# Attention pipeline: evictions of keys and queries at the head of a step, conversions of values behind the result, products dealt nine and six

## The chip, the core and the metric

The kernel runs on one core of a Trainium2 chip. TensorE (PE in the profile; PEld is its weight load) multiplies matrices into PSUM, VectorE (DVE) and ScalarE (ACT) read PSUM and work element by element, GpSimd (POOL) works on SBUF and issues some of the DMAs, SyncE (SP) issues the other DMAs. Each engine runs its own queue strictly in order; a semaphore makes one wait for another. The metric is the device time of one execution in microseconds. Before the change it was 2920.61 us, the median of three runs (2917.56 to 2922.97).

## The reference

Two layers of a backbone over 1024 latent tokens and 256 context tokens, 1024 channels each. The first layer mixes with Fourier groups and long convolutions, the second with neighbourhood attention; each ends in a SwiGLU feed-forward part. Only the attention of the second layer matters here. 16 heads of 64 channels; a query sees an 8 x 16 window of keys on a grid of 16 rows by 64 columns, with a bias by relative position, and all context keys:

```python
s_loc = einsum("bcqhd,bicjhd->bhcqij", q_r, k_b) * scale + bias
s_loc = where(col_ok, s_loc, -inf)
s_ctx = einsum("bcqhd,bjhd->bhcqj", q_r, kc) * scale
p = softmax(concatenate([s_loc, s_ctx], axis=-1))
o = einsum("bhcqij,bicjhd->bcqhd", p_loc, v_b) + einsum("bhcqj,bjhd->bcqhd", p_ctx, vc)
```

## The kernel before, in words

Operands are kept as a high and a low half in a narrower type, so that one product of the reference becomes three matmuls (high by high, high by low, low by high).

The attention has 64 items: 8 pairs of heads (`pr`), two halves of the rows (`hf`), four groups of 16 columns (`c`). An item has 128 queries, 384 local keys and 256 context keys for each of its two heads. One step of the loop over `k` in `attention` works on three items at once:

- `attn_scores` and `attn_softmax` for item k + 1: twelve score matmuls into four PSUM banks named `sc`; then on DVE the smallest context score (L2072), the sum with the bias and its extremum (L2074), on ACT the exponentials (L2078, L2080). The context half is split by ACT (L2086) and POOL (L2087) and transposed by a DMA on SyncE's queue (L2088).
- `attn_turn` for item k: PE transposes the local half (L2098) into two banks named `tr`; `turned` copies it out, high half on ACT (L2107), low half on DVE (L2110).
- `attn_values` for item k - 1: thirty matmuls with the values, into the unused half of a score bank of item k + 1 (`free`); then DVE takes the reciprocal of the softmax sum (L2138) and multiplies (L2139) into `osb`. Only then is that score bank free for the scores of the next step. Every fourth step `attn_send` transposes a finished `osb` (L2150), splits it (L2152 on ACT, L2153 on DVE) and stores it. From item 52 on, the context half is transposed on PE too, in `attn_late`.

Between these pieces PE does the projections of the next pair: `attn_prep` is a generator that yields after every three matmuls into one of two accumulators `pq`. Five accumulations of 24 matmuls make a pair: two of the keys (512 columns), the context keys (256), two of the queries (512). `fetch(target)` draws from this generator until the work drawn reaches the target. For the last eight steps and beyond, the generator is the output projection (`first_part`).

What ACT and DVE have to do for the projections is not done on the spot but put in a list, `self.later`, by `later(work)`: the **evictions** of a finished accumulator (`key`: copy on ACT L300 and rest on DVE L302; `context_key`: L1946 and L1947; `query`: L1951 and L1952), and the **conversions** of a loaded group of values (`value`: POOL memset L1973, ACT L1974, DVE L1975; no DMA). An eviction is listed when the generator is drawn from again after its last product; a conversion at a fixed count of products. `flush()` empties the list.

The loop lies in a `manual_schedule`: the queues of PE, ACT, DVE and POOL hold the instructions in the order in which the code issues them.

Of the kernel before, what the change touches and what calls it, by code (L numbers as in the profile page):

```python
# [201 lines left out]
class Builder:  # L202
# [1705 lines left out]
    def attn_prep(self, pr, u):  # L1908

        nc = self.nc  # L1910
        kh, kl = self.S4(F32R), self.S4(F32R)
        kc = self.S2(F32R)
        qs, vt, staged = {}, [], {}
        loads, turns = (1, 5, 10, 16, 22), (12, 16, 22, 28, 33)
        step = 0

        def lin(wh, wl, pc, view=lambda x: x):
            nonlocal step, acc
            yield None
            acc = self.PQ()  # L1920
            for kb in range(KB):
                for w, part in ((wh, 0), (wh, 1), (wl, 0)):
                    self.mm(acc[:, :WID[pc]], w[:, kb * P:(kb + 1) * P], view(u.ap(part, kb, pc)),
                            kb == 0 and w is wh and part == 0, kb == KB - 1 and w is wl)
                step += 1
                for c in range(5):
                    if step == loads[c]:
                        load(c)
                    if step == turns[c]:
                        later(lambda c=c: value(c))  # L1930
                yield WID[pc] / 1024

        def by_chunk(x):
            return x.rearrange("p (r h c) -> p h r c", r=8, h=4)

        def later(work):
            if pr == 0:
                work()
            else:
                self.later.append(work)  # L1940

        def key(acc, cols):
            self.split(acc, kh[:, cols], kl[:, cols])

        def context_key(acc):
            nc.scalar.mul(kc[:, :256], acc[:, :256], -1.0)  # L1946
            nc.vector.scalar_tensor_tensor(kc[:, 256:], acc[:, :256], -1.0, kc[:, :256].bitcast(F32), op0=MUL, op1=SUB)  # L1947

        def query(acc, pc):
            qh, ql = qs[pc] = self.S2(F32R), self.S2(F32R)  # L1950
            nc.scalar.mul(qh, acc, self.qinv)  # L1951
            nc.vector.scalar_tensor_tensor(ql, acc, self.qinv, qh.bitcast(F32), op0=MUL, op1=SUB)  # L1952

        def load(c):
            st = staged[c] = self.T()
            if c < 4:
                src = self.vd[0:LAT].rearrange("(g r w) c -> r w g c", g=4, r=4)
                for r in range(4):
                    self.ld(st[r * 32:r * 32 + 32].rearrange("p (g c) -> p g c", g=4),
                            src[r, KSTART[c]:KSTART[c] + 32, :, pr * P:(pr + 1) * P])  # L1960
            else:
                self.ld(st[:, :256].rearrange("p (j c) -> p j c", j=2),
                        self.vd[LAT:LAT + CTX, pr * P:(pr + 1) * P].rearrange("(j p) c -> p j c", j=2))

        def value(c):
            st = staged.pop(c)
            w = 512 if c < 4 else 256
            n = w // 64
            t = self.S4(F16, 2048) if c < 4 else self.S2(F16, 1024)
            v = t[:, :66 * n].rearrange("p (k c) -> p k c", c=66)  # L1970
            lo = t[:, 66 * n:130 * n]
            src = st[:, :w].rearrange("p (k c) -> p k c", c=64)
            nc.gpsimd.memset(v[:, :, 64:65], 1.0)  # L1973
            nc.scalar.activation(v[:, :, :64], src, AF.Copy, scale=self.vs)  # L1974
            nc.vector.scalar_tensor_tensor(lo.rearrange("p (k c) -> p k c", c=64), src, self.vs, v[:, :, :64],  # L1975
                                           op0=MUL, op1=SUB)
            vt.append((v, lo))

        acc = None
        wk = self.halves_of("wk", 0) if pr == 0 else self.aw  # L1980
        for pc in (0, 1, 2):
            if pc == 1:
                wq = self.halves_of("wq", pr)
            yield from lin(*wk, pc)
            later((lambda acc=acc: context_key(acc)) if pc == 2 else
                  (lambda acc=acc, pc=pc: key(acc, slice(pc * 512, pc * 512 + 512))))
        for pc in (0, 1):
            if pc == 1 and pr < 7:
                self.aw = self.halves_of("wk", pr + 1)
            yield from lin(*wq, pc, by_chunk)  # L1990
            later(lambda acc=acc, pc=pc: query(acc, pc))
        self.prep[pr] = (qs, (kh, kl), (kc[:, :256], kc[:, 256:]), vt)
        yield 0.1

    def attention(self, u, fill):
        self.prep, self.osb, self.aw, self.later, self.turns = {}, {}, None, [], []
        self.od = [[self.DR([P, LAT], F16) for _ in range(2)] for _ in range(8)]
        self.accumulators(sc=4, tr=2, pq=2)
        n = sum(x or 0 for x in self.attn_prep(0, u))
        prep = (x for pr in range(1, 9) for x in (self.attn_prep(pr, u) if pr < 8 else fill))  # L2000
        items = [(pr, hf, c) for pr in range(8) for hf in (0, 1) for c in range(4)]
        state = [{} for _ in items]
        done = 0

        def piece(step, k):
            if 0 <= k < 64:
                step(state[k], *items[k])

        def fetch(target):
            nonlocal done  # L2010
            while done < target:
                done += next(prep) or 0

        def flush():
            while self.later:
                self.later.pop(0)()

        for k in range(2):
            piece(self.attn_bias, k)
        e = mybir.EngineType  # L2020
        with self.tc.manual_schedule(engines={e.PE, e.Activation, e.DVE, e.Pool}):
            for k in range(-1, 65):
                piece(self.attn_bias, k + 3)
                piece(self.attn_send, k - 2)
                piece(self.attn_scores, k + 1)
                piece(self.attn_turn, k)
                piece(self.attn_softmax, k + 1)
                flush()
                fetch((k * 3 + 8.5) * n / 24)
                free = state[k + 1]["free"] if k + 1 < 64 else self.SC()[:, 256:]  # L2030
                if 0 <= k - 1 < 64:
                    self.attn_values(state[k - 1], *items[k - 1], free)
                piece(self.attn_late, k)
                flush()
                fetch((k * 3 + 10) * n / 24)
            flush()
            piece(self.attn_send, 63)
        for _ in prep:
            pass
        self.accumulators(pp=6, pq=2)  # L2040
# [524 lines left out]
```

## Time and profile before

| | us |
|---|---|
| median of three runs | 2920.61 |
| the profiled execution, its own time | 2916.52 |
| its span in the trace | 2914.8 |
| six whole rounds of eight steps (1815.4 to 2124.1) | 51.4 each |
| PE, DVE, ACT busy in the round 1918.3 to 1969.7 | 48.67, 34.50, 31.53 |
| DMA share and PE clock granted in that round | 0.65, 1.00 |

The profiled execution is one run; its span is the time between its first and last instruction, and 1.7 us lie around it. A busy engine is one that has an instruction in work; PE's matmuls overlap, so the profile models their ends. The attention loop is some 410 us of the span.

### The profile page before, as it was taken

The page shows a single profiled execution, that of the slowest core. Times are in us where ns is not written, and L with a number is a line of the kernel's source. Part 1 is how long each engine was busy: PE and PEld are TensorE (multiplying, and loading weights), DVE is VectorE, ACT ScalarE, POOL GpSimd, SP SyncE. Part 2 cuts the span into 40 slices and gives each one's busy share as a digit, 9 for nine tenths or more (in the row PEclk, how much of TensorE's full clock was granted, in tenths as well). Part 3 has the DMA queues.
Part 4 walks back from the last instruction along what each step waited for, and adds up shares of the span by engine and source line. Part 5 has one row for each costly group of instructions (what it writes and reads, how often), then busy time and mean ns, then how long its engine had stood idle before and what let it go on. Part 6 is the DMA issues. An engine that isn't in the chain of part 4 may idle for free. (4 is left out here: it accounts for less than half of the span.)

```text
span 2914.8 us, 46336 instructions
## 1 busy us (share of the span) xinstructions
PE 2761.7 (95%) x16419; PEld 1686.2 (58%) x16419; DVE 2078.8 (71%) x3857; ACT 1619.3 (56%) x2857; POOL 593.3 (20%) x977
## 2 busy tenths in 40 slices
PE   6989999999989999999999999999999999999998
PEld 3755557888879544444555844666665444444554
DVE  4778767575467898877886766666675778765755
ACT  4674325454675676654465655666663467554543
POOL 1012013354121121112120012333331012112000
PEclk8999999999999999999999999999999999999999
DMA  7574435359695655556994897666664656424753
GB/s 258 189 272 169 157 114 169 108 175 307 248 356 176 208 217 195 210 195 255 321 321 161 300 336 276 147 164 154 164 189 163 231 215 239 154 99 179 235 189 124
DMA packets 323362, 607.58 MB, mean 208 GB/s; under 512 B 89910, under 2 KB 131576, under 8 KB 323130
## 3 DMA queue, kind: packets, MB, share of 16 engines
q1 hardware_dynamic: 254682, 387.53, 40.6%
q0 software_dynamic: 66144, 212.91, 20.6%
q10 hardware_dynamic: 2304, 4.20, 0.4%
q8 instruction: 128, 2.10, 0.3%
q14 instruction: 104, 0.85, 0.1%
HBM read 455.33 MB, written 135.53 MB: 203 GB/s over the span
## 5 line engine op out<-in xcount | busy, mean ns | idle before, releaser
L1462 PE MATMUL ps<-s,s 128*128 128x512 f16 x2244 | 507.4, 381 | 8.6 <-ACT tk L1467 4.2
L1462 PEld LDWEIGHTS <-s 128*128 128x128 f16 x2640 | 258.6, 98 | 330.7 <-issue 25.2
L296 PE MATMUL ps<-s,wh 128*128 128x256 f32 (+3 forms) x1764 | 400.8, 330 | 12.4 <-ACT wh L300 5.4
L1231 ACT ACTIVATE s<-s,c 128x512 f16<-128x512 f32 (+1 forms) x324 | 233.6, 752 | 149.2 <-DMA s<-d 73.5
L1232 DVE SCALAR_TENSOR_TENSOR s<-s,c,s 128x512 f16<-128x512 f32 (+1 forms) x324 | 247.2, 793 | 90.1 <-ACT s L1231 89.3
L1679 PE MATMUL ps<-s 128*128 128x512 f16 (+2 forms) x1308 | 303.6, 378 | 2.0 <-DVE s L1232 2.0
L296 PE MATMUL pq<-s,wh 128*128 128x512 f16 (+1 forms) x988 | 273.6, 355 | 5.0 <-DMA wh<-d 3.0
L296 PE MATMUL ps<-s,wl 128*128 128x256 f32 (+3 forms) x882 | 263.6, 331 | 2.5 <-DVE wl L302 1.2
L1679 PEld LDWEIGHTS <-s 128*128 128x128 f16 x1536 | 148.5, 98 | 179.0 <-issue 6.8
L296 PEld LDWEIGHTS <-wh 128*128 128x128 f16 x1664 | 159.6, 99 | 152.6 <-issue 13.6
L287 POOL DMA_DIRECT2D d<-s x201 | 108.7, 541 | 640.6 <-DVE s L1523 182.5
L348 ACT CAST mat<-cs 128x1024 fp32r<-128x1024 f16 (+2 forms) x120 | 111.5, 934 | 137.7 <-PE ps L296 56.6
L296 PEld LDWEIGHTS ps<-s,wh 128*128 128x128 f32 x1088 | 177.1, 192 | 18.1 <-ACT wh L300 5.7
L296 PE MATMUL ps<-s,mat 128*128 128x512 f32 x696 | 180.5, 405 | 4.6 <-DVE s L302 4.3
L1462 PE MATMUL ps<-s,wh 128*128 128x512 f16 x608 | 182.2, 379 | 1.7 <-DVE g L1476 1.3
L296 PE MATMUL pq<-s,wl 128*128 128x512 f16 (+1 forms) x494 | 172.3, 354 | 0.0
L296 PE MATMUL sc<-s,s 128*128 128x65 f16 (+3 forms) x2688 | 153.2, 233 | 16.6 <-DVE s L2139 13.3
L296 PEld LDWEIGHTS <-s 128*128 128x128 f16 x2400 | 113.2, 98 | 80.0 <-issue 11.5
L296 PEld LDWEIGHTS ps<-s,mat 128*128 128x128 f32 x696 | 133.3, 194 | 38.5 <-DVE s L302 5.5
L1264 ACT ACTIVATE t<-s 128x1024 bf16<-128x1024 f32 (+1 forms) x164 | 141.5, 863 | 12.3 <-DVE c L483 8.5
L2107 ACT CAST s<-tr 128x384 f16<-128x384 f32 (+1 forms) x140 | 62.9, 490 | 137.2 <-PE tr L2098 136.9
L296 PEld LDWEIGHTS <-wl 128*128 128x128 f16 x832 | 82.2, 99 | 81.5 <-issue 2.8
(435 smaller groups left out, 5555.6 us busy)
## 6 DMA issues: line engine op xcount, KB each, us to landing
s<-d SPq DMA_DIRECT2D x294, 256.0 KB, 4.4
d<-s POOLq DMA_DIRECT2D x157, 256.0 KB, 3.5
s<-in_down SPq DMA_DIRECT2D x154, 256.0 KB, 5.1
s<-in_ada_w POOLq DMA_DIRECT2D x48, 512.0 KB, 4.7
s<-in_gate SPq DMA_DIRECT2D x46, 512.0 KB, 3.9
s<-in_up SPq DMA_DIRECT2D x46, 512.0 KB, 4.3
d<-g POOLq DMA_DIRECT2D x87, 256.0 KB, 3.5
d<-tk POOLq DMA_DIRECT2D x82, 256.0 KB, 4.5
```

The costliest lines, as they stand in the source:

```text
L287: self.last_ldr = self.nc.gpsimd.dma_start(out, in_).ins
L296: return self.nc.tensor.matmul(o, l, r, start=st, stop=sp).ins
L348: self.nc.scalar.copy(m, st)
L1231: nc.scalar.activation(hi, src, AF.Copy, scale=scale)
L1232: nc.vector.scalar_tensor_tensor(lo, src, scale, hi, op0=MUL, op1=SUB)
L1264: self.nc.scalar.activation(junk[:, :t.shape[1]], t, AF.Abs, scale=2.0 ** -15, accum_out=st[:, k:k + 1])
L1462: nc.tensor.matmul(ps, x[:, sl], y, start=first and j == 0 and x is wh and y is xh, stop=j == 3 and x is wl, skip_group_check=True)
L1679: m = nc.tensor.matmul(acc[j][:, c0:c1], x[:, sl], y[:, xs], start=first and k == 0, stop=last and k == 2, skip_group_check=True)
L2107: self.nc.scalar.copy(t[:, :w], ps[:, :w])
```

## The change

Three edits in the order of a step, and a second list.

- The conversions of values go to a list of their own, `self.casts`.
- `flush(self.later)`, now the evictions alone, opens a step, ahead of `attn_send` and the scores. Before, the list was emptied behind the softmax and once more at the end of the step.
- `flush(self.casts)` stands behind `attn_values`, ahead of `attn_late`.
- The first `fetch` of a step goes to `k * 3 + 8.9` instead of `k * 3 + 8.5`; the second is unchanged.

```diff
                     if step == turns[c]:
-                        later(lambda c=c: value(c))
+                        later(lambda c=c: value(c), self.casts)
...
-        def later(work):
+        def later(work, queue=self.later):
             if pr == 0:
                 work()
             else:
-                self.later.append(work)
+                queue.append(work)
...
-        def flush():
-            while self.later:
-                self.later.pop(0)()
+        def flush(queue):
+            while queue:
+                queue.pop(0)()
...
             for k in range(-1, 65):
                 piece(self.attn_bias, k + 3)
+                flush(self.later)
                 piece(self.attn_send, k - 2)
                 piece(self.attn_scores, k + 1)
                 piece(self.attn_turn, k)
                 piece(self.attn_softmax, k + 1)
-                flush()
-                fetch((k * 3 + 8.5) * n / 24)
+                fetch((k * 3 + 8.9) * n / 24)
                 free = state[k + 1]["free"] if k + 1 < 64 else self.SC()[:, 256:]
                 if 0 <= k - 1 < 64:
                     self.attn_values(state[k - 1], *items[k - 1], free)
+                flush(self.casts)
                 piece(self.attn_late, k)
-                flush()
                 fetch((k * 3 + 10) * n / 24)
-            flush()
+            flush(self.later)
+            flush(self.casts)
```

Two lines come in ahead of the loop, so L2072 to L2153 of before are L2074 to L2155 of the changed kernel.

Where the conversions and evictions stand is seen on DVE. Here is its queue from the end of the softmax of one step to the beginning of the next, in the step of a round in which a conversion of values and the second half of the keys meet (`tr` are the transposed weights, `t` the loaded values, `sc` a score bank with a result or with scores, `pq` a projection). Before:

```order
L2110 TENSOR_TENSOR s_4177_19681<-tr_19668,s_4177_19681 128x384
L2110 TENSOR_TENSOR s_4178_19683<-tr_19672,s_4178_19683 128x384
L1975 SCALAR_TENSOR_TENSOR s_4181_19697<-t_19418,c_17518,s_4181_19697 128x512
L2138 RECIPROCAL st_19457<-sc_19654 128x2
L2139 TENSOR_TENSOR s_4183_19711<-sc_19654,st_19457 128x128
L302 TENSOR_TENSOR s_4110_19310<-pq_19485,s_4109_19309 128x512
L2072 TENSOR_REDUCE st_19791<-sc_19769 128x1
```

The same place now:

```order
L2112 TENSOR_TENSOR s_4177_19681<-tr_19668,s_4177_19681 128x384
L2112 TENSOR_TENSOR s_4178_19683<-tr_19672,s_4178_19683 128x384
L2140 RECIPROCAL st_19457<-sc_19654 128x2
L2141 TENSOR_TENSOR s_4182_19710<-sc_19654,st_19457 128x128
L1975 SCALAR_TENSOR_TENSOR s_4183_19743<-t_19386,c_17518,s_4183_19743 128x512
L302 TENSOR_TENSOR s_4110_19310<-pq_19485,s_4109_19309 128x512
L2074 TENSOR_REDUCE st_19791<-sc_19769 128x1
```

The two instructions of the division have passed the conversion; the eviction L302 stands between the conversion and the reduction, as it did.

Three steps later a query and the short last conversion stood together ahead of the division. DVE's queue there, before:

```order
L2110 TENSOR_TENSOR s_4085_19141<-tr_19128,s_4085_19141 128x384
L2110 TENSOR_TENSOR s_4086_19143<-tr_19132,s_4086_19143 128x384
L1952 SCALAR_TENSOR_TENSOR s_4090_19158<-pq_18956,c_13658,s_4089_19157 128x512
L1975 SCALAR_TENSOR_TENSOR s_4091_19161<-t_18895,c_17518,s_4091_19161 128x256
L2138 RECIPROCAL st_18931<-sc_19114 128x2
L2139 TENSOR_TENSOR s_4039_18851<-sc_19114,st_18931 128x128
```

Now:

```order
L2112 TENSOR_TENSOR s_4087_19145<-tr_19132,s_4087_19145 128x384
L2112 TENSOR_TENSOR s_4088_19147<-tr_19136,s_4088_19147 128x384
L2140 RECIPROCAL st_18931<-sc_19118 128x2
L2141 TENSOR_TENSOR s_4038_18850<-sc_19118,st_18931 128x128
L1975 SCALAR_TENSOR_TENSOR s_4091_19202<-t_18893,c_17518,s_4091_19202 128x256
```

The conversion has gone behind the division, and the query's L1952 has left this place for the head of the step, ahead of the reduction L2074.

The dealing of the products is seen on PE, at the end of the first fetch of a step (`pq` products, then the values into `sc`). Before, the sixth product is the last:

```order
L296 LDWEIGHTS wl_19482
L296 MATMUL pq_19816<-s_3363_15495,wl_19482 128x512
L296 LDWEIGHTS s_4177_19681
L296 MATMUL sc_19769<-s_4037_18837,s_4177_19681 128x65
L296 LDWEIGHTS s_4177_19681
```

Now three more follow, up to the ninth:

```order
L296 LDWEIGHTS wl_19482
L296 MATMUL pq_19812<-s_3363_15495,wl_19482 128x512
L296 LDWEIGHTS wh_19481
L296 MATMUL pq_19812<-s_3368_15512,wh_19481 128x512
L296 LDWEIGHTS wh_19481
L296 MATMUL pq_19812<-s_3368_15512,wh_19481 128x512
L296 LDWEIGHTS wl_19482
L296 MATMUL pq_19812<-s_3368_15512,wl_19482 128x512
L296 LDWEIGHTS s_4177_19681
L296 MATMUL sc_19769<-s_4039_18883,s_4177_19681 128x65
```

Counted over a round, four steps had six products ahead of the values and nine behind and now have nine and six. The step of the context keys, whose products have 256 columns and half the length, had nine and fifteen and now has twelve and twelve. The other three keep six and six.

More of the change, by code (lines that the diff above doesn't have):

```diff
@@ L1995, in attention @@
     def attention(self, u, fill):
-        self.prep, self.osb, self.aw, self.later, self.turns = {}, {}, None, [], []
+        self.prep, self.osb, self.aw, self.turns = {}, {}, None, []
+        self.later, self.casts = [], []
         self.od = [[self.DR([P, LAT], F16) for _ in range(2)] for _ in range(8)]
```

## The prediction

> **What bounds the kernel now.** I began with the page: the whole execution, and how busy each engine is.
>
> ```profile
> span 2914.8 us, 46336 instructions
> PE 2761.7 (95%) x16419; PEld 1686.2 (58%) x16419; DVE 2078.8 (71%) x3857; ACT 1619.3 (56%) x2857; POOL 593.3 (20%) x977
> ```
>
> TensorE (PE) is 95% busy, so a change of order can only win what holds PE up. The change lies in attention alone, which by the first and last score products runs from about 1805 to 2215 us. Second view: what PE waited for in that stretch (columns: who waited, for whom, us in total, times, longest).
>
> ```profile
> PE sc L296 <- DVE s L2139: 13.3, 21, 0.9
> PE tr L2150 <- DVE s L2139: 3.5, 6, 0.6
> PE sc L296 <- ACT t L2078: 3.3, 11, 0.4
> ```
>
> Nearly everything is a wait for L2139, the division of a result by its softmax sum on VectorE (DVE). It stands 21 + 6 times; with seven pairs of heads being prepared that is three or four times in each round of eight steps. Third view: the timeline of such a round (start us, length, engine, line; in brackets the idle time ahead and what ended it). A round is the distance between the first and the fifth row here, 1918.30 - 1866.85 = 51.45 us.
>
> ```profile
> 1866.85 1.06 PE L296 MATMUL sc<-s,s 128*128 128x65 f16 x30 [0.23 <-ACT t L2078]
> ...
> 1916.40 0.74 DVE L2072 TENSOR_REDUCE st<-sc 128x1 f32<-128x256 f32 x2
> ...
> 1917.06 0.61 DVE L2074 CUSTOM_DVE_ANT_0 g<-sc,g,st 128x384 f32<-128x384 f32 x1
> ...
> 1917.78 0.47 ACT L2078 ACTIVATE t<-sc,st 128x256 f32<-128x256 f32 x1 [0.17 <-DVE st L2074]
> ...
> 1918.30 1.06 PE L296 MATMUL sc<-s,s 128*128 128x65 f16 x30 [0.23 <-ACT t L2078]
> ...
> 1920.78 1.13 DVE L1975 SCALAR_TENSOR_TENSOR s<-t,c,s 128x512 f16<-128x512 f32 x1 [1.63 <-ACT s L1974]
> ...
> 1920.93 0.79 PE L296 MATMUL sc<-s,s 64*128 64x256 f32 x7
> ...
> 1921.83 0.16 DVE L2138 RECIPROCAL st<-sc 128x2 f32<-128x2 f32 x1
> ...
> 1922.02 0.29 DVE L2139 TENSOR_TENSOR s<-sc,st 128x128 f32<-128x128 f32 x1
> 1922.23 0.68 DVE L302 TENSOR_TENSOR s<-pq,s 128x512 fp32r<-128x512 f32 x1
> ...
> 1922.46 0.77 PE L296 MATMUL sc<-s,s 64*128 64x384 f32 x5 [0.74 <-DVE s L2139]
> 1922.83 0.74 DVE L2072 TENSOR_REDUCE st<-sc 128x1 f32<-128x256 f32 x2
> ...
> 1923.16 0.55 PE L2098 MATMUL tr<-c,g 128*128 128x128 f32 x3
> ...
> 1923.87 0.59 PE L296 MATMUL pq<-s,wh 128*128 128x512 f16 x2
> ```
>
> The weighted values begin on PE at 1918.30; their result could be divided about a microsecond later. But the conversion L1975 is ahead of L2138 in DVE's queue, sat 1.63 us until ScalarE (ACT) had its half L1974 done, and ran 1.13 us. So L2138 starts at 1921.83, and the scores, whose bank L2139 has to free, stop after seven of twelve products until 1922.46. What such a stop really costs needs a step without one, which follows with the two other stopped scores of the round (1928.11 and 1934.19) and the head of a step that sends a result (1941.48).
>
> ```profile
> 1924.49 0.49 ACT L2078 ACTIVATE t<-sc,st 128x256 f32<-128x256 f32 x1
> ...
> 1926.73 0.74 ACT L1974 ACTIVATE s<-t,c 128x512 f16<-128x512 f32 x1
> ...
> 1927.51 1.13 DVE L1975 SCALAR_TENSOR_TENSOR s<-t,c,s 128x512 f16<-128x512 f32 x1 [1.93 <-ACT s L1974]
> ...
> 1928.11 0.80 PE L296 MATMUL sc<-s,s 64*128 64x256 f32 x7
> ...
> 1928.96 0.41 DVE L1947 SCALAR_TENSOR_TENSOR s<-pq,s 128x256 fp32r<-128x256 f32 x1
> ...
> 1929.29 0.74 DVE L2072 TENSOR_REDUCE st<-sc 128x1 f32<-128x256 f32 x2
> ...
> 1929.89 0.55 PE L2098 MATMUL tr<-c,g 128*128 128x128 f32 x3
> ...
> 1934.19 0.80 PE L296 MATMUL sc<-s,s 64*128 64x256 f32 x7
> ...
> 1936.62 0.55 PE L2098 MATMUL tr<-c,g 128*128 128x128 f32 x3
> ...
> 1940.95 0.75 DVE L1952 SCALAR_TENSOR_TENSOR s<-pq,c,s 128x512 fp32r<-128x512 f32 x1 [2.20 <-ACT s L1951]
> ...
> 1941.48 0.49 PE L2150 MATMUL tr<-c,s 128*128 128x128 f32 x3
> ...
> 1946.04 1.06 PE L296 MATMUL sc<-s,s 128*128 128x65 f16 x30
> ...
> 1947.21 0.17 DVE L2138 RECIPROCAL st<-sc 128x2 f32<-128x2 f32 x1 [0.32 <-PE sc L296]
> ...
> 1948.33 1.16 PE L296 MATMUL sc<-s,s 64*128 64x256 f32 x12
> ...
> 1948.99 0.76 DVE L2072 TENSOR_REDUCE st<-sc 128x1 f32<-128x256 f32 x2 [1.28 <-PE sc L296]
> ...
> 1949.42 0.55 PE L2098 MATMUL tr<-c,g 128*128 128x128 f32 x3
> ...
> 1950.13 0.59 PE L296 MATMUL pq<-s,wh 128*128 128x512 f16 x2
> ...
> 1951.43 1.07 PE L296 MATMUL sc<-s,s 128*128 128x65 f16 x30
> ...
> 1952.33 0.59 PE L296 MATMUL pq<-s,wh 128*128 128x512 f16 x2
> ...
> 1954.37 1.44 PE L296 MATMUL sc<-s,s 64*128 64x256 f32 x12
> ```
>
> An undisturbed step, from 1948.33: scores to transposes 1.09 us, to the first products 1.80; six products to 1951.43 (1.30, so 0.215 each, nine 1.94); values to the next products 0.90; then nine products and 0.10 to the next scores (2.04 in all). Scores to transposes take 2.23 us at 1920.93, 1.78 at 1928.11, 2.43 at 1934.19, so the three stops cost 1.14, 0.69 and 1.34. The waits row shows only 13.3 / 21 = 0.63 each, because a matmul's modelled end runs on into the stop.
>
> The Trainium skill says the same on its page "Perfetto Trace Analysis", section "Identifying the Most-Contended Engine": matmul busy time misjudges the headroom, since instructions in the pipeline overlap. By the shown idle time the removable part would be 16.8 us in all; the starts above, which decide here, give more.
>
> **The change, part by part.** Number the steps of a round 0 to 7, the values at 1918.30 being step 1. The order of the program shows four edits.
>
> *Conversions go behind the division.* L2138 and L2139 pass L1975 (and its ACT half no longer gates them). Values at V give L2138 at V + 1.17 (1946.04 to 1947.21), and the scores are free 0.63 after L2138 (1921.83 to 1922.46): V + 1.80. PE is at the gated product at V + 0.90 + six products 1.29 + 0.10 + 7/12 of 1.09 = V + 2.93. About 1.1 us are spare, so the three stops go: 1.14 + 0.69 + 1.34 = 3.17 us in a round. The fourth wait, the send at 1941.48, stands behind L1952 and the short conversion; both leave its path, and I count its shown 3.5 / 6 = 0.58. Removed: 3.75 us a round.
>
> *Evictions open the step.* L302, L1947 and L1952 now stand at the head of DVE's queue, ahead of the send's copy and of the reduction L2072, and their ACT halves ahead of the copies of the transposes. Queued behind them is the whole softmax, and PE's values wait for its first exponential, L2078. For the key and the context key this is no new place: L302 and L1947 already stand just ahead of L2072 in the rows above. The query's L1952 does come new ahead of it. What is late next is therefore the ring L2078, L1974, L1975, eviction, L2072, L2074, L2078: 2.24 (1924.49 to 1926.73) + 0.78 + 1.05 (1920.78 to 1921.83) + eviction + 0.66 (1916.40 to 1917.06) + 0.72 = 5.45 us and the eviction, 0.60 for L302 (to 1922.83), 0.33 for L1947 (to 1929.29), at most 0.75 for L1952: rings of 6.05, 5.78 and 6.20 into steps 2, 3 and 4.
>
> *Nine and six.* With nine products ahead of the values and six behind, PE's own time from values to values is 0.90 + 1.29 + 0.10 + 1.80 + 1.94 = 6.03; with six and six 5.39. Steps 0, 2, 4, 6 are of the first kind, the others of the second. The total of products is the same.
>
> Ring against PE, from L2078 of step 1 at T, values at T + 0.52 (1917.78 to 1918.30): into step 2 the ring needs 6.05, PE 6.03, equal. But the next query's first product needs the accumulator that L302 empties: L302 ends at T + 2.24 + 0.78 + 1.05 + 0.68 = T + 4.75, PE is there at T + 0.52 + 4.09 = T + 4.61, so it waits 0.2 with the signal's way; values at T + 6.77. Step 3: ring T + 11.83 and 0.52 makes T + 12.35, PE T + 12.16: 0.2 lost. Step 4: ring T + 18.55, PE T + 18.38: 0.2 lost. New holds: 0.6 us a round. In step 5 the send and a short conversion meet as before; I take nothing. Bounds: 0 if the ring is a little faster than these rows, 1.5 if each link of the three steps is 0.3 later.
>
> The Trainium skill ("Perfetto Trace Analysis", section "Matmuls") speaks against this edit: independent groups should rotate through banks so that emptying one overlaps the next group's products. There are two such banks here, and before the change L302 ended (1922.91) 0.96 us ahead of 1923.87; this spare time is what the edit spends. The price is the 0.2 above.
>
> *Loads and POOL.* The order on the SyncE queue is the same; one load of values is asked for at the end of nine products instead of after three more behind the values. POOL's memset stays between the same two pieces. Steps come faster, by less than 10%, so the softmax transposes by DMA have slightly less time; no wait of PE for a DMA is among the three rows above. Taken as nothing, with 0 to 2 us for both ends together.
>
> **Sum.** A round wins 3.75 - 0.6 = 3.15 us. Six whole rounds make 18.9; of the seventh, where a third transpose joins and other work follows, I count the first two stops, 1.8: 21 us. From the other side: PE alone needs 4 x 6.03 + 4 x 5.39 = 45.7 and about 0.9 for two sends, 46.6 us against 51.45; if all of the 4.9 goes but 0.6, six rounds and 2 us make 28. I take 23, nearer to the sum of named rows. The profiled execution took 2916.5 us (its span and 1.7 us around it), 4.1 less than the median 2920.6. Its time would become 2893.5, the median's 2897.6; I predict **2896**.
>
> **Rivals.** (1) *Only the shown idle time counts*, because the tail of a modelled matmul is real work: 16.8 us less 0.6 x 7 and a further 0.2 per step on the ring, about 11 us won, 2908. For it: the waits row. Against it: the starts, which leave 4.9 us in a round unexplained by PE's work. (2) *The ring sets the pace anyway*: if values follow values in steps 2 to 4 by 6.7 us as at 1918.30 and after, nothing moves, 2915 to 2926. Against it: the ring sums to 5.8 to 6.2, and L1975's 1.63 and 1.93 us of idle ahead show that DVE is not short of time. (3) *Slower*: evictions at the head hold L2072 by their own time and by the conversion's, 1.05 + 0.60, in steps 1, 2, 3, 4 and 6 with nothing to absorb it: 8.2 us in a round against 3.75 won, 30 us lost, 2950. It decides from the point where L2072 comes over 1.15 us (nine products) or 0.5 us (six) after its natural place, 0.66 behind the scores, by about 0.8 us more in each step; the ring gives 1.2 and 0.7, just over the edge, not far over. (4) *All holds vanish*: 30 us won or more, 2886.
>
> **Chances.** Forecast (18 to 29 us won) 0.60; rival 1 (6 to 18) 0.20; rival 2 0.09; rival 3 0.07; rival 4 0.04. A measurement of this kernel tells about 0.2%, 6 us, from no change. So faster 0.84, same 0.09, slower 0.07. The range runs from rival 4 to the weak end of rival 1: 2886 to 2914.
>
> **What would show it.** PE's waits for the division gone or under 2 us in attention; L2138 about 1.2 us after the values in each step; scores to transposes 1.09 in steps 2 to 4; a round of 47 to 48.5 us; new short waits of PE for L302 (products) once a round and for L2078 (values) in steps 3 and 4. Wrong would be: waits of values for L2078 of over 0.5 us in most steps (rival 3), or a round near 51 with no wait shown (rival 2).

## The result and the profile after

The changed kernel takes 2896.97 us, the median of four runs (2894.54 to 2899.26); the kernel before, with one more run, 2921.79 us. The ratio is 0.992, 95% interval 0.9901 to 0.994: faster by 0.6 to 1.0%. The prediction was 2896, range 2886 to 2914.

The page of the profiled execution (its own time 2897.7 us), and what PE waited for in the attention:

```profile
span 2895.6 us, 46377 instructions
PE 2758.4 (95%) x16419; PEld 1688.7 (58%) x16419; DVE 2081.9 (72%) x3857; ACT 1620.2 (56%) x2857; POOL 593.0 (20%) x977
```

```profile
PE sc L296 <- ACT t L2080: 2.4, 5, 1.0
PE tr L2100 <- DVE s L2112: 1.1, 1, 1.1
PE sc L296 <- DMA s<-s: 0.8, 1, 0.8
```

Not one wait for the division (now L2141) is left; before there were 27. Of the 2.4 us for the exponential L2080, 2.2 lie in the last steps, behind 2120. The timeline from step 1 to step 4 of a round, and the values of the next step 1:

```profile
1915.20 1.06 PE L296 MATMUL sc<-s,s 128*128 128x65 f16 x30
...
1916.37 0.17 DVE L2140 RECIPROCAL st<-sc 128x2 f32<-128x2 f32 x1 [0.32 <-PE sc L296]
...
1917.50 1.16 PE L296 MATMUL sc<-s,s 64*128 64x256 f32 x12
...
1917.68 1.13 DVE L1975 SCALAR_TENSOR_TENSOR s<-t,c,s 128x512 f16<-128x512 f32 x1 [0.76 <-ACT s L1974]
...
1918.59 0.55 PE L2100 MATMUL tr<-c,g 128*128 128x128 f32 x3
1918.73 0.68 DVE L302 TENSOR_TENSOR s<-pq,s 128x512 fp32r<-128x512 f32 x1
...
1919.33 0.74 DVE L2074 TENSOR_REDUCE st<-sc 128x1 f32<-128x256 f32 x2
...
1919.46 0.59 PE L296 MATMUL pq<-s,wh 128*128 128x512 f16 x2
...
1920.22 0.62 DVE L2076 CUSTOM_DVE_ANT_0 g<-sc,g,st 128x384 f32<-128x384 f32 x1
...
1920.88 0.47 ACT L2080 ACTIVATE t<-sc,st 128x256 f32<-128x256 f32 x1 [0.85 <-DVE st L2076]
...
1921.41 1.06 PE L296 MATMUL sc<-s,s 128*128 128x65 f16 x30
...
1927.17 1.06 PE L296 MATMUL sc<-s,s 128*128 128x65 f16 x30 [0.22 <-ACT t L2080]
...
1933.20 1.07 PE L296 MATMUL sc<-s,s 128*128 128x65 f16 x30
...
1962.57 1.06 PE L296 MATMUL sc<-s,s 128*128 128x65 f16 x30
```

L2140 follows the values by 1.17 us, with the conversion L1975 behind it instead of ahead. The twelve score products run through, and the transposes come 1.09 us behind the scores (1917.50 to 1918.59) where they took 2.23 before. This round is 1962.57 - 1915.20 = 47.37 us, 4.08 less than the 51.45 read before. It is not the typical one: the six whole rounds take 47.14, 47.13, 47.37, 47.13, 47.13 and 48.07 us (the last with a wait for a DMA in it). Their median is 47.13, which is 4.31 less than before, where all six take 51.44 or 51.45. Here are exponentials and values of the next round, from the exponential that its step 1 waits for to the values of step 3, and the values of the step 1 after it:

```profile
1962.05 0.47 ACT L2080 ACTIVATE t<-sc,st 128x256 f32<-128x256 f32 x1 [0.17 <-DVE st L2076]
...
1968.02 0.47 ACT L2080 ACTIVATE t<-sc,st 128x256 f32<-128x256 f32 x1 [0.62 <-DVE st L2076]
...
1968.78 1.07 PE L296 MATMUL sc<-s,s 128*128 128x65 f16 x30
...
1973.78 0.47 ACT L2080 ACTIVATE t<-sc,st 128x256 f32<-128x256 f32 x1 [0.18 <-DVE st L2076]
...
1974.30 1.06 PE L296 MATMUL sc<-s,s 128*128 128x65 f16 x30
...
2009.70 1.06 PE L296 MATMUL sc<-s,s 128*128 128x65 f16 x30
```

What is left are two small holds of PE. Into step 2 the ring of ScalarE and VectorE takes 1968.02 - 1962.05 = 5.97 us, but the values come 6.21 behind those of step 1 (1962.57) and 0.76 behind the exponential: it is PE that sets the pace there, with a short wait for the accumulator (see "The accumulator" below). Into step 3 the values follow the exponential by 0.52, the distance that they had before the change where PE waited for it (1917.78 to 1918.30). There the ring sets the pace, with 5.76 us, and PE loses 0.14. In the round shown first the ring into step 2 took 6.21, because L2076 followed L2074 by 0.89 us and not by 0.66 or 0.67 as in the other five; so that round lost 0.37 in step 3. The change once more, the change without the dealing and the kernel with more products in the last steps have the same delay in their third round too; no run shows why.

The whole loop, by the first and the last product into a score bank, before and after:

```profile
L296 PE MATMUL sc<-s,s x2688: 190/194/445, 1798.7 to 2214.3; 128*128 128x65 f16 x126, 64*128 64x256 f32 x64, 128*128 128x64 f16 x2
```

```profile
L296 PE MATMUL sc<-s,s x2688: 189/194/413, 1804.2 to 2192.5; 128*128 128x65 f16 x126, 64*128 64x256 f32 x64, 128*128 128x64 f16 x2
```

415.6 us became 388.3: the loop is 27.3 us shorter, though the profiled executions are only 18.8 apart (2916.5 and 2897.7). 5.5 us of the difference lie ahead of the loop, in a part that the change does not touch, the rest behind it; the experiments show how far the part ahead scatters.

### The profile page after: what moved, and what is told of

Same layout as the page of the kernel before. It is cut to its first block, busy times and chain, and to the rows that moved or that the text cites. A ratio compares the mean times of both kernels' runs of the same rounds, so it can differ in the third digit from the quotient of the medians.

```text
span 2895.6 us, 46377 instructions
## 1 busy us (share of the span) xinstructions
PE 2758.4 (95%) x16419; PEld 1688.7 (58%) x16419; DVE 2081.9 (72%) x3857; ACT 1620.2 (56%) x2857; POOL 593.0 (20%) x977
## 5 line engine op out<-in xcount | busy, mean ns | idle before, releaser
L296 PE MATMUL sc<-s,s 128*128 128x65 f16 (+3 forms) x2688 | 142.6, 231 | 3.2 <-ACT t L2080 2.4
L1231 ACT ACTIVATE s<-t,c 128x512 f16<-128x512 f32 x172 | 115.2, 712 | 21.9 <-DVE c L1330 9.3
```

What stands on the lines that cost most here:

```text
L296: return self.nc.tensor.matmul(o, l, r, start=st, stop=sp).ins
L1231: nc.scalar.activation(hi, src, AF.Copy, scale=scale)
```

## The experiments

The question was which of the three edits wins the time, whether the ring is what paces the steps now, and whether anything is left to win. A round is measured from the values of one step 1 to those of the next, the loop as above. The table has the third of the six whole rounds, which is the one of the rows shown, and the median of the six.

| kernel | median us | ratio, 95% interval | third round us | median round us | loop us |
|---|---|---|---|---|---|
| before | 2921.79 | | 51.44 | 51.44 | 415.6 |
| the change | 2896.97 | 0.992 (0.9901 to 0.994) | 47.37 | 47.13 | 388.3 |
| conversions alone | 2900.59 | 0.9934 (0.9918 to 0.9951) | 48.09 | 48.09 | 393.8 |
| evictions alone | 2916.05 | 0.9993 (0.9975 to 1.001) | 50.91 | 50.90 | 412.1 |
| dealing alone | 2919.49 | 0.9995 (0.9978 to 1.0013) | 51.17 | 51.16 | 413.7 |
| change without dealing | 2896.80 | 0.9927 (0.9905 to 0.995) | 48.14 | 47.90 | 392.3 |
| VectorE's half of evictions twice | 2909.91 | 0.9947 (0.9927 to 0.9967) | 49.28 | 49.47 | 403.8 |
| conversions' low half on POOL | 2895.71 | 0.9901 (0.9884 to 0.9919) | 46.84 | 46.84 | 384.9 |
| more products in the last steps | 2894.58 | 0.9902 (0.9888 to 0.9917) | 47.38 | 47.17 | 391.1 |
| two low halves behind the softmax | 2896.55 | 0.9911 (0.9894 to 0.9928) | 47.00 | 47.00 | 386.2 |
| POOL and last steps together | 2887.42 | 0.9886 (0.9861 to 0.9911) | 46.85 | 46.84 | 387.7 |
| the change, once more | 2896.72 | 0.9933 (0.991 to 0.9956) | 47.39 | 47.14 | 387.8 |

Each ratio is against runs of the kernel before that stood beside it (medians 2918.60 to 2923.29), so it is not the quotient of the medians shown. Whole kernels can't tell effects of under 0.2% apart. Median rounds and loops, which repeat to 0.01 and 0.5 us in the two profiles of the change, can.

### Conversions alone

```diff
                 piece(self.attn_bias, k + 3)
-                flush(self.later)
...
                 piece(self.attn_softmax, k + 1)
-                fetch((k * 3 + 8.9) * n / 24)
+                flush(self.later)
+                fetch((k * 3 + 8.5) * n / 24)
...
                 flush(self.casts)
                 piece(self.attn_late, k)
+                flush(self.later)
```

> Only the conversions go behind the division; the evictions stand where they stood before (behind the softmax and at the end of a step) and the products are dealt 6 and 9. Theory (the gain comes from the division passing the conversions): the three stopped scores of a round go (1.17, 0.69 and 1.33 us), the send waits some 0.3 us in place of 0.94 because the query's eviction is still ahead of the division, and the six products ahead of the values leave the ring into step 2 uncovered (0.5 us). Round 48.1 us against 51.4 before and 47.4 with the whole change; first score to last score about 21 us shorter than before, against 27.3 for the whole change. Rival A (the evictions at the head of the step carry the gain): round above 50. Rival B (the nine and six carry it): round above 50.

PE's waits for the division, L2142 in this kernel, first for the send and then for the scores, and two rows of values a round apart:

```profile
PE tr L2153 <- DVE s L2142: 1.1, 6, 0.2
...
PE sc L296 <- DVE s L2142: 0.4, 1, 0.4
```

```profile
1916.72 1.06 PE L296 MATMUL sc<-s,s 128*128 128x65 f16 x30 [0.23 <-ACT t L2081]
...
1964.81 1.06 PE L296 MATMUL sc<-s,s 128*128 128x65 f16 x30 [0.23 <-ACT t L2081]
```

48.09 us, as expected; the loop is 21.8 us shorter, four fifths of the whole gain. The stops of the scores are gone but for one of 0.4 us, and the send's small wait is there. Neither rival holds.

### Evictions alone

```diff
                 piece(self.attn_softmax, k + 1)
-                fetch((k * 3 + 8.9) * n / 24)
+                flush(self.casts)
+                fetch((k * 3 + 8.5) * n / 24)
...
-                flush(self.casts)
                 piece(self.attn_late, k)
+                flush(self.casts)
```

> Only the evictions go to the head of a step; conversions stay behind the softmax and at the end of a step, ahead of the division, and the products are dealt 6 and 9. Theory: the query's L1952 leaves the path of the send (0.94 us a round) and that of the scores of step 7 (0.27), the three stops behind the conversions stay. Round 50.2 us, attention loop about 7 us shorter than before. Rival A (evictions carry the gain): round 48 to 49.

50.91 us, less than half of the expected gain, the loop 3.5 us shorter instead of 7. The rival is further off still, but the expectation for the send missed. The timeline at the send shows why:

```profile
1938.41 1.15 POOL L2090 TENSOR_TENSOR s<-t,s 128x512 f16<-128x512 f32 x1 [4.51 <-ACT s L2089]
1938.83 1.02 DVE L1975 SCALAR_TENSOR_TENSOR s<-t,c,s 128x256 f16<-128x256 f32 x1 [1.72 <-issue]
1939.49 0.49 PE L2153 MATMUL tr<-c,s 128*128 128x128 f32 x3
1939.77 0.16 DVE L2141 RECIPROCAL st<-sc 128x2 f32<-128x2 f32 x1
...
1940.31 0.33 PE L2153 MATMUL tr<-c,s 128*128 128x128 f32 x1 [0.33 <-DVE s L2142]
```

With L1952 out of the way the short conversion runs earlier, beside POOL's split L2090, and takes 1.02 us; before, behind L1952, it took 0.48. So the division is only some 0.25 us earlier. The send needs both edits: from its step to the next the values take 7.41 us before, 7.16 here, 7.01 with the conversions alone, and 6.60 in the change without the dealing. The rest of the gain, 0.28, is the hold of the scores in step 7, which is gone as expected.

### Dealing alone

```diff
-                fetch((k * 3 + 8.5) * n / 24)
+                fetch((k * 3 + 8.9) * n / 24)
```

> The kernel before with the products dealt nine and six alone. Theory: the stopped scores are released by the chain of ScalarE and VectorE (exponential, conversion, division), which does not depend on when PE reaches the values, so the three products only move from behind the values into the wait: stops grow by what the values come later. Round 51.4 plus or minus 0.3, loop within 2 us of before. Rival B (the nine and six carry the gain): round below 50.

Values of step 1, of step 2 and of the next step 1:

```profile
1919.30 1.06 PE L296 MATMUL sc<-s,s 128*128 128x65 f16 x30
...
1926.82 1.07 PE L296 MATMUL sc<-s,s 128*128 128x65 f16 x30
...
1970.47 1.06 PE L296 MATMUL sc<-s,s 128*128 128x65 f16 x30
```

51.17 us, 0.28 less than before. From step 1 to step 2 it now takes 7.52 us where it took 6.87: the stop stands where it stood, and the three products moved ahead of the values come on top; the next steps give it back. The 0.28 is the same hold of step 7: into that step the values come 0.94 us sooner, where the moved products alone make 0.65.

### The change without the dealing

```diff
-                fetch((k * 3 + 8.9) * n / 24)
+                fetch((k * 3 + 8.5) * n / 24)
```

> The whole change but for the dealing (6 and 9 as before). Theory: the rings through conversion and eviction into steps 2 and 4 (6.2 and 6.0 us as measured in the changed kernel) are longer than PE's own 5.7 and 5.4 there, holds of 0.5 and 0.35 us; step 1 holds the values by 0.5 us as before the change. Round 47.9 us against 47.4, loop about 4 us longer than with the whole change, waits of the values for L2080 shown three times a round. Rival B (nine and six carry the gain): round above 49.

Values of steps 1, 2 and 4, and of the next step 1:

```profile
1915.21 1.06 PE L296 MATMUL sc<-s,s 128*128 128x65 f16 x30 [0.23 <-ACT t L2080]
...
1921.42 1.06 PE L296 MATMUL sc<-s,s 128*128 128x65 f16 x30 [0.31 <-ACT t L2080]
...
1933.34 1.06 PE L296 MATMUL sc<-s,s 128*128 128x65 f16 x30 [0.34 <-ACT t L2080]
...
1963.35 1.06 PE L296 MATMUL sc<-s,s 128*128 128x65 f16 x30 [0.23 <-ACT t L2080]
```

48.14 us in the round shown and 47.90, as expected, in the five others; the loop is 4.0 us longer than with the whole change. The waits stand in the steps that were named, but that of step 2 only in the round shown (18 waits in the whole loop, five of them behind the sixth round): in the others the ring into step 2 takes 5.97 us. Nine and six is a cover for the ring, worth 0.77 us a round once the division is free (47.90 against 47.13), and 0.28 by itself. By whole kernels it can't be seen (2896.80 and 2896.97).

The three parts alone win 3.35, 0.54 and 0.28 us of a median round, 4.17 together; the whole change wins 4.31.

### Is the ring the pace? VectorE's half of the evictions twice

```diff
             self.split(acc, kh[:, cols], kl[:, cols])
+            nc.vector.tensor_tensor(kl[:, cols], acc, kh[:, cols].bitcast(F32), SUB)
...
+            for _ in (0, 1):
-            nc.vector.scalar_tensor_tensor(kc[:, 256:], acc[:, :256], -1.0, kc[:, :256].bitcast(F32), op0=MUL, op1=SUB)
+                nc.vector.scalar_tensor_tensor(kc[:, 256:], acc[:, :256], -1.0, kc[:, :256].bitcast(F32), op0=MUL, op1=SUB)
...
+            for _ in (0, 1):
-            nc.vector.scalar_tensor_tensor(ql, acc, self.qinv, qh.bitcast(F32), op0=MUL, op1=SUB)
+                nc.vector.scalar_tensor_tensor(ql, acc, self.qinv, qh.bitcast(F32), op0=MUL, op1=SUB)
```

> The whole change, with VectorE's half of each eviction written twice (same numbers into the same place). Theory (what paces the conversion steps now is the ring exponential, conversion, eviction, reduction, exponential): the rings into steps 2, 3 and 4, measured 6.21, 5.76 and 6.03 us, grow by the second write, 0.60, 0.33 and 0.66; nothing grows in steps 0 and 6, where the accumulation ended long before. Round 47.4 + 1.6 = 49.0, loop some 10 us longer than with the whole change. Rival (VectorE has room, PE paces): loop under 2 us longer.

Values of steps 1 and 2 and of the next step 1, and two of PE's waits, for the emptied accumulator and for the softmax weights that a DMA transposes:

```profile
1927.35 1.06 PE L296 MATMUL sc<-s,s 128*128 128x65 f16 x30
...
1934.29 1.07 PE L296 MATMUL sc<-s,s 128*128 128x65 f16 x30
...
1976.63 1.06 PE L296 MATMUL sc<-s,s 128*128 128x65 f16 x30
```

```profile
PE pq L296 <- DVE s L1944: 5.2, 7, 0.7
PE sc L296 <- DMA s<-s: 2.2, 3, 1.4
```

49.28 us against 49.0 expected. The six rounds take 49.11 to 50.65, the shortest 1.98 more than the change's 47.13, for 1.59 us of added work. The loop grew by 15.5 us, more than the 10 expected: some 2 us in each round, and 2.2 us of waits for DMAs, which were not foreseen. So VectorE has no room in these steps, and the query's first product does wait for the accumulator (L1944 is the second write of the key's low half), seven times, once a round.

### Conversions' low half on POOL

```diff
-            nc.vector.scalar_tensor_tensor(lo.rearrange("p (k c) -> p k c", c=64), src, self.vs, v[:, :, :64],
-                                           op0=MUL, op1=SUB)
+                nc.gpsimd.tensor_scalar(src, src, self.vs, None, op0=MUL)
+                nc.gpsimd.tensor_tensor(lo.rearrange("p (k c) -> p k c", c=64), src, v[:, :, :64], SUB)
```

(for the pairs that are prepared in the loop; the first pair keeps the instruction of before)

> The whole change, with the low half of a conversion made on POOL in two instructions (scale in place, subtract) instead of L1975 on VectorE. Theory: the ring loses L1975, 1.05 us, and comes below PE's own time in steps 2, 3 and 4, so the holds of 0.18, 0.37 and about 0.1 go and the wait for the accumulator with them: round 46.7 against 47.4, loop 4.5 us shorter than with the whole change. Rival: POOL's two instructions of about 1.2 us each stand ahead of the next step's split L2089 and of the bias loads; the context half then comes late from its transpose by DMA, and the values wait for a DMA in most rounds: loop the same or longer.

POOL behind the values of a step 1, and two rows of values a round apart:

```profile
1920.99 1.17 POOL L2093 TENSOR_TENSOR s<-t,s 128x512 f16<-128x512 f32 x1 [1.18 <-ACT s L2092]
...
1922.18 1.57 POOL L1979 TENSOR_SCALAR t<-t,c 128x512 f32<-128x512 f32 x1
1923.84 1.12 POOL L1980 TENSOR_TENSOR s<-t,s 128x512 f16<-128x512 f32 x1
```

```profile
1919.08 1.06 PE L296 MATMUL sc<-s,s 128*128 128x65 f16 x30
...
1965.92 1.06 PE L296 MATMUL sc<-s,s 128*128 128x65 f16 x30
```

46.84 us, 0.3 less than with the change by the median round (0.7 expected), and close to what PE needs by itself (46.6 by the estimate in the prediction). POOL gets the 2.7 us done within the step, and no wait for a DMA appears in the loop, so the rival falls. The loop is 3.4 us shorter than with the change (4.5 expected). Into step 2 the values now take 6.04 us (1919.08 to 1925.12) instead of 6.21, into step 3 5.38 instead of 5.53: both holds are gone.

### More products in the last steps

```diff
                         load_o(kb, (0,), self.ld)
-                        yield 1
+                        yield 0.3
```

> The whole change; the output projection's generator counts 0.3 instead of 1 for a load without products, so that steps 54 to 57 get more products (of the 13 us' worth that come after the loop anyway). Theory: in these steps three products are too few to cover the exponentials, and the four or five waits of the values for L2080 (2.4 us shown, some 3 by the starts) go; whole kernel 2 to 3 us shorter, loop longer by the products that move into it. Rival: the steps are held by the third transpose and its copies, and nothing changes.

The waits for the exponential shrink from 2.4 us to one:

```profile
PE sc L296 <- ACT t L2080: 0.2, 1, 0.2
```

The loop is 2.8 us longer, since products moved into it. The median is 2.4 us below the change's, within the noise of whole kernels: the waits are shown to go, the gain in time is not shown by this run alone.

### Two low halves behind the softmax

L1947 and L1952 go to a third list, emptied behind the softmax; ScalarE's halves stay at the head.

```diff
                 piece(self.attn_softmax, k + 1)
+                flush(self.halves_due)
```

> The whole change, but VectorE's half of the evictions of the context keys and the queries (L1947, L1952) goes behind the softmax of the same step, ahead of the division; ScalarE's half stays at the head. Theory: the rings into steps 3 and 4 lose 0.33 and 0.66 us; the hold of 0.37 in step 3 goes, step 4 has next to none to lose; the division comes up to 0.75 us later, which the 1.1 us of spare time take. Round 47.0, loop 2 to 3 us shorter. Rival: the division in the query's step becomes late again and the scores stop: round above 47.5.

Values of steps 1, 2 and 3, and of the next step 1:

```profile
1915.93 1.06 PE L296 MATMUL sc<-s,s 128*128 128x65 f16 x30
...
1922.14 1.07 PE L296 MATMUL sc<-s,s 128*128 128x65 f16 x30
...
1927.52 1.07 PE L296 MATMUL sc<-s,s 128*128 128x65 f16 x30
...
1962.93 1.06 PE L296 MATMUL sc<-s,s 128*128 128x65 f16 x30
```

47.00 us as expected, though only 0.13 less than the change's median round: step 2 to step 3 takes 5.38 us, PE's own time, where the change takes 5.53 (5.76 in the round shown). The division is not late at all: L2143 still follows the values by 1.17 us (1933.56 to 1934.73 in the query's step), since the low half ends before the values do.

### Together, beside the change once more

> The whole change with two additions that were looked at apart: a conversion's low half on POOL, and 0.3 in place of 1 for a load without products. Theory: the loop wins the 0.5 us a round and the waits of the last steps at once, 6 us together against the whole change, of which the part behind the loop may give some back in waits for the projection's weights: 2890 to 2894 us. Rival (what follows the loop takes it all): 2896.

> The changed kernel as it is, on the same chip beside the other. Theory: 2896 to 2898 us; in the profile the loop takes 388.3 us again and a round 47.4, while the part ahead of the loop starts it anywhere between 1797 and 1811 us, as it did in the kernels so far.

The edits of "conversions' low half on POOL" and "more products in the last steps" in one kernel take 2887.42 us, ratio 0.9886 (0.9861 to 0.9911), 3 us below the expected stretch; its round is 46.85 us and no wait for an exponential is left in the loop. The change itself, on the same chip, takes 2896.72 us, ratio 0.9933 (0.991 to 0.9956), with a loop of 387.8 us and a round of 47.39, 47.14 by the median. The combined kernel is ahead of the change; its lead over the two kernels with one addition each, run on another chip, is not shown, as the intervals overlap. Why it wins 9 us and not the 6 of the sum was not settled. Its four runs span 2879 to 2891, and by the profiles it needs 7.7 us less from the loop's first product to the end. The loops are equal there, and what follows takes 695.3 us instead of 702.9; it has fewer products to do, but it also scatters, from 697.4 to 703.9 over the ten profiles with the same work behind the loop.

## Why the prediction was right

**The bound and the mechanism** held. The waits for the division were the conversion's place in VectorE's queue: moving it alone wins four fifths of the loop's gain, and the three stops go to the 1.09 us that were read from an undisturbed step. L2140 comes 1.17 us behind the values, as forecast.

**The size by starts, not by shown idle time.** Rival 1, 11 us, is refuted by the loop's 27.3. The trap is there again after the change. A round of 47.13 us in the view by stretches (us, then the busy time of PE, PEld, DVE, ACT and POOL, the clock, the DMA share and GB/s):

```profile
1868.07:1915.20 47.13, 47.13 (x514) 31.40 (x512) 35.18 (x93) 31.85 (x69) 18.80 (x31) 1.00 0.78 171
```

PE seems busy all the time, and still 0.3 us came out of a round when the conversion's low half went to POOL. The rule of the Trainium skill that was weighed there ("Perfetto Trace Analysis", "Identifying the Most-Contended Engine") agrees with this trace.

**The term that was mis-sized** is "removed: 3.75 us a round". It took the send at its shown 0.58; by the starts the send took 1.33 us (1941.48 to 1942.81), where an undisturbed one took 0.53 (1914.54 to 1915.07), so its hold was 0.80. It also left out the small holds of the values in step 1 and of the scores in step 7 (0.39 and 0.28 by the starts). With these the removed part is 4.64 us. The new holds were put at 0.6, three of 0.2; measured are 0.17 in step 2, 0.14 in step 3 and none in step 4. 4.64 - 0.31 = 4.33 is what the median round won, 4.31, against 3.15 forecast by the named rows and 4.3 from the other side. Six rounds won 24.7 us (the wait for a DMA and the longer third round are in them) and the rest of the loop 2.6, where 1.8 was forecast: 27.3 against the 21 of the sum and the 23 that was taken. The medians of the whole kernel differ by 24.8.

**Rings.** From values to values into steps 2, 3 and 4 I had 6.25, 5.58 and 6.20 us; measured are 6.21, 5.53 and 6.03 in five of six rounds. From exponential to exponential the ring was summed to 6.05, 5.78 and 6.20; it took 5.97, 5.76 and 6.03. So the ring alone holds PE in step 3 only: into step 2 it would be ready first, and into step 4 it and PE come out even. Rival 2, the ring as the pace in any case, and rival 3, the ring so long that the kernel is slower, are refuted; with the evictions' work doubled the ring does cost 2 us a round, so the edge was as near as it was put. Rival 4, no holds left, falls with the 0.31 that are left.

**The accumulator.** The key's L302 ends at 1919.41, and the query's first product comes at 1919.46, 0.87 behind the transposes instead of 0.71: 0.16 lost, 0.2 forecast. The trace lists no wait there, because the transposes' modelled end (1918.97 and 0.49) covers it. Two experiments show that it is this wait: with the conversion's low half on POOL, L302 comes sooner and the 0.17 of step 2 is gone, and with the evictions doubled it is listed. The rule of the Trainium skill on rotating banks that spoke against the edit ("Perfetto Trace Analysis", section "Matmuls") is borne out in kind by the doubled evictions, where the same product waits 5.2 us in seven rounds.

**Loads and the rest.** One wait for a softmax transpose by DMA, 0.8 us, which I had taken as nothing. That the time was met within 1 us is partly luck. The working ended at 2897.6, and the 2896 of the forecast has no reason beside it; 23 was a choice between 21 and 28; the sum was 4 us short for the loop, and 2.5 of these don't appear in the median.

## What to carry to other kernels

Where an engine with an in-order queue serves both the path of the busiest engine and work that only has to be done some time, put the first ahead of the second, above all when the second waits for a third engine: the waiting instruction blocks everything behind it. Price a stop by the distance between starts of the same two instructions in a disturbed and an undisturbed step, not by the idle time shown. Moving products to cover a wait helps little when the wait moves along with them: here it won 0.28 us a round alone and 0.77 once the order was changed. Compare several rounds before reading a hold from one: a single late instruction made the round shown here 0.24 us longer than its neighbours and its ring look like the pace.

## What the runs showed of the hardware that was not expected

- The short conversion (128 x 256, two inputs in SBUF) takes 0.48 us by itself and 1.02 beside a subtraction of POOL; the long one 0.75 (at 2139.49 before the change) and 1.13. Beside POOL's issuing of a DMA, as at 1941.61 before the change, the short one keeps its 0.48. The Trainium skill's page "GPSIMD Engine Reference", section "Specifications", states that POOL shares its SBUF interfaces with VectorE and contends with instructions of two SBUF inputs; the trace agrees.
- The part ahead of the loop, the same program in all kernels but the one with doubled evictions (1810.9 us there), brought the loop's first product at 1797.8 to 1808.9 us over the eleven other profiles. The clock granted in the first 400 us was 0.94 in the five kernels that were there by 1802.7 and 0.91 to 0.93 in the seven that came later, and 1.00 in the loop in all; that the clock makes the difference was not tried apart. Stages can be compared to some tenths of a microsecond between profiles, whole executions only to several.
- The transposes by DMA landed 3.9 to 6.8 us after their issue before and 4.1 to 8.5 after the change (median 5.4 in both), and PE waited for one of them, 0.8 us, only after the change. That the shorter steps have used up what was spare for the slowest is likely but not shown: other kernels with steps as short (46.84 and 47.00) have no such wait.
